# An SSD branch whose heads begin beside its convolution, in a two-layer hybrid encoder

## The chip, the cores and the metric

The kernel runs on one core of one Trainium2 chip. Its engines work side by side: TensorE (PE) multiplies matrices, VectorE (DVE) and ScalarE (ACT) work elementwise, GpSimd (POOL) does little here, and SyncE (SP) issues the transfers (DMAs). Each engine takes its instructions in a fixed order and waits where an operand is not there yet. The metric is the device time of one launch in microseconds (us), lower is better.

## What is computed

Two layers act on x of 512 tokens by 2048 features, in float32. Each one normalises, multiplies by one wide input matrix whose columns go to two branches, and multiplies the joined branches by one output matrix; a gate made from the conditioning vector scales the sum into x. The first layer (attention and S5) is not touched. The second, cut to what matters:

```python
h, gate = ada_modulate(x, c, norm_g, ada_w, ada_b)        # gate: a 2048 x 2048 product with silu(c)
q, k, v, g_c, z, xbc, dt_raw = split_cols(h @ w_in, ...)
o_c = neighbourhood_attention(q, k, v, rpb) * silu(g_c)   # 8 heads of 128
# SSD: 16 heads of 64, 2 groups of B and C with 128 states, chunks of 128 tokens, two directions
xbc = silu(depthwise_conv_centred(xbc, conv_w, conv_b))   # 5 taps, 1536 channels: x 1024, B 256, C 256
scores = einsum('bclhn,bcshn->bhcls', C, B) * exp(segsum(dt * a))
y_diag = einsum('bhcls,bcshp->bclhp', scores, x * dt)      # inside a chunk, head by head
states = ...                                               # B^T x per chunk, carried from chunk to chunk
y_off = einsum('bclhn,bchpn->bclhp', C, states) * exp(a_cum)
o_d = rms_norm((y_fwd + y_bwd + d * x) * silu(z), norm_w)
out = concat(o_c, o_d) @ w_out;  x = x + gate * out
```

## The kernel before

Every large product is done as three float32r matmuls: the operand and the weight are each split into a high and a low part, `wh` by a copy on ACT (L128), `wl` by a subtraction on DVE (L129). Weights come in pieces of 512 KB, in the order of a list (`plan1`), through two buffers `w` and three of `wh` and `wl`. PE works in units. A `tunit` is 48 matmuls of 128x512 (L167 to L169) into one of four banks `m`; a `runit` (L234 to L236) gives a whole 512x256 result.

Layer 1 issues: three runits for z and dt; twelve tunits for the convolution's channels (x0 to x7, B, C); eight tunits for the gate of the attention; then twelve runits, k, v and q of four pairs of heads; then sixteen output units. The runits of k, v and q read a reordered copy of h; its first tile is a copy into the buffer G11, high half on ACT (L1764), low half on DVE (L1765), and the others go into freed tiles of h.

Everything else is in streams, Python generators of which `slot` takes a step after every twelve or so matmuls. Their instructions are issued with raised priority, and a list scheduler of the framework, which knows the priorities and simulates times, fixes each engine's order when the kernel is built. The streams of layer 1:

- `ada_stream((3,), G[7:9])`: the gate of layer 1, 32 pieces of 512 KB through the two tiles G7 and G8, each multiplied and summed on DVE (L629). `finish("dt", "conv", "ada3")` ends it before the gate's tunits.
- `dt_stream`: step sizes, cumulative sums, and rows of decays, stored to DRAM (`csd`).
- `conv_stream`: for each of the twelve units five taps (L1322, L1325), tanh (L1330), a product (L1333), and for x and B transposes on PE (L1337) with a copy (L1339).
- `ssd`, started after all twelve units: `ssd_heads` loads a head's rows of decays (DMAs from `csd`), takes exponentials on ACT (L1392, L1394), multiplies on DVE (L1402, L1406 eight times, L1410) and multiplies by x on PE (L1416); `ssd_states` carries the states, per group of heads and per direction three steps of two PE products (L1446, L1455) with DVE products between them (L1443, L1451, L1452, L1458, L1459); `ssd_end` multiplies by the gate z (L1468), normalises, and stores the result to DRAM (`odd`).
- `na_stream`: the attention, one step a slot, which waits for the end of `ssd`.

After the last runit `odd` is loaded (L1796) and split, and the output units begin with the SSD half.

Of the kernel before, what the change touches and what calls it, by code (L numbers as in the profile page):

```python
# [66 lines left out]
class Trunk:  # L67
    def __init__(self, tc, ctx, A):
        self.tc, self.nc, self.A = tc, tc.nc, A
        self.sb = ctx.enter_context(tc.tile_pool(name="sb", bufs=1))  # L70
        self.pp = ctx.enter_context(tc.tile_pool(name="pp", bufs=1, space=PSUM))
        self.dr = ctx.enter_context(tc.tile_pool(name="dr", bufs=1, space=DRAM))
        self.uid = 0
        self.streams = []
        self.mrot = self.trot = 0
        self.nmain = 4
        self.sstep = 1
        self.flags = set()

    def nm(self, p):  # L80
# [23 lines left out]

    def slot(self, hold=()):
        for _ in range(self.sstep):
            for st in list(self.streams):
                if st[0] in hold:
                    continue
                for _ in range(st[2]):  # L110
                    with self.tc.high_priority(offset=PRI_BG):
                        r = next(st[1], "end")
                    if r == "end":
                        self.streams.remove(st)
                        self.flags.add(st[0])
                        break
# [1078 lines left out]
    def dt_stream(self, raw, G):  # L1195
# [29 lines left out]
        n = 8  # L1225
# [28 lines left out]
        for i, (part, at, al) in enumerate(((hi, 3, 4), (lo, 5, 6))):  # L1254
# [48 lines left out]
    def conv_stream(self, xins, G, xs):  # L1303
# [10 lines left out]
        acc = self.sl(G[9], [128, 2, 512])  # L1314
        tnh = self.sl(G[10], [128, 2, 512])
        for i in range(13):
            if i < 12:
                j = i
                yield from self.wait(f"xin{j}")
                xin = xins.pop(j)  # L1320
                a = acc[:, j % 2]
# [7 lines left out]
                tn = tnh[:, j % 2]  # L1329
                nc.scalar.activation(out=tn, in_=a, func=AF.Tanh)  # L1330
                dst = self.bT[:, j - 8] if 8 <= j < 10 else self.cT[:, j - 10] if j >= 10 else a
                yield
                nc.vector.scalar_tensor_tensor(out=dst, in0=tn, scalar=1.0, in1=a, op0=ALU.add, op1=ALU.mult)  # L1333
                if j < 10:
                    tp = self.bank("b3")
                    for t in range(4):
                        nc.tensor.transpose(tp[:, t * 128:t * 128 + 128], dst[:, t * 128:t * 128 + 128], self.ident)  # L1337
                    o = xs[:, :, j * 128:j * 128 + 128] if j < 8 else self.bs[:, :, (j - 8) * 128:(j - 8) * 128 + 128]
                    nc.scalar.copy(out=o, in_=tp.rearrange("p (t c) -> p t c", t=4))  # L1339
            yield  # L1340

    def ssd_heads(self, G, xs, ys):
# [42 lines left out]
        pd = None  # L1385
        for i in range(16 + 1):
            if i < 16:
                h = i
                r = rt[h].rearrange("p d (c l) -> p d c l", c=4)
                for d in range(2):  # L1390
# [5 lines left out]
                nc.scalar.activation(out=ys[:, :, x], in_=xs[:, :, x], func=AF.Identity, scale=self.ssd_dd[:, h:h + 1])  # L1396
            yield
            h = i - 1
            if h >= 0:
                e, lo = rt.pop(h), rl.pop(h)  # L1400
# [10 lines left out]
                load(h + 3)  # L1411
                if h % 2 == 0:
                    pd = self.bank("b1")
                for c in range(4):
                    o = (h % 2) * 256 + c * 64
                    nc.tensor.matmul(out=pd[:, o:o + 64], lhsT=wp[:, h % 2, c * 128:c * 128 + 128],  # L1416
                                     rhs=xs[:, c, h * 64:h * 64 + 64])
                if h % 2 == 1:
                    yo = ys[:, :, (h - 1) * 64:(h + 1) * 64].rearrange("p c (h x) -> p c h x", h=2)
                    v.tensor_tensor(out=yo, in0=pd.rearrange("p (h c x) -> p c h x", h=2, c=4), in1=yo, op=ALU.add)  # L1420
                    self.flags.add(f"yd{h // 2}")
            yield

    def ssd_states(self, G, xs, ys):

        nc = self.nc
        v = nc.vector
        dv = self.dtv
        xo = self.sl(G[10], [128, 2, 512])
        sp = self.sl(G[9], [128, 2, 512])  # L1430
        n = 0
        for g in range(2):
            yield from self.wait(f"yd{4 * g + 3}")
            for d in range(2):
                hs = slice(16 * d + 8 * g, 16 * d + 8 * g + 8)
                cols = slice(g * 512, g * 512 + 512)
                hv = lambda t: t.rearrange("p (h x) -> p h x", h=8)
                bc = lambda t: t.unsqueeze(2).to_broadcast([128, 8, 64])
                order = (0, 1, 2, 3) if d == 0 else (3, 2, 1, 0)
                for i in range(3):  # L1440
                    c, c2 = order[i], order[i + 1]
                    x = xo[:, 0]
                    v.tensor_tensor(out=hv(x), in0=hv(xs[:, c, cols]), in1=bc(dv["dec"][:, c, hs]), op=ALU.mult)  # L1443
                    yield
                    ps = self.bank("b2")
                    nc.tensor.matmul(out=ps, lhsT=self.bs[:, c, g * 128:g * 128 + 128], rhs=x)  # L1446
                    s, sl = sp[:, i % 2], sp[:, 1 - i % 2]
                    if i == 0:
                        nc.scalar.copy(out=s, in_=ps)
                    else:  # L1450
                        v.tensor_tensor(out=hv(s), in0=hv(sl), in1=bc(dv["etot"][:, c, hs]), op=ALU.mult)  # L1451
                        v.tensor_tensor(out=s, in0=s, in1=ps, op=ALU.add)  # L1452
                    yield
                    po = self.bank("b3")
                    nc.tensor.matmul(out=po, lhsT=self.cT[:, g, c2 * 128:c2 * 128 + 128], rhs=s)  # L1455
                    yield
                    o = xo[:, 1]
                    v.tensor_tensor(out=hv(o), in0=hv(po), in1=bc(dv["ecs"][:, c2, hs]), op=ALU.mult)  # L1458
                    v.tensor_tensor(out=ys[:, c2, cols], in0=ys[:, c2, cols], in1=o, op=ALU.add)  # L1459
                    n += 1  # L1460

# [192 lines left out]
    def layer1(self):  # L1654
# [72 lines left out]
        for j in range(12):  # L1727
            def ev(ps, j=j):
                t = self.sl(G[14 + j % 2], [128, 516])
                nc.gpsimd.memset(t[:, 0:2], 0.0)  # L1730
                nc.gpsimd.memset(t[:, 514:516], 0.0)
                nc.scalar.copy(out=t[:, 2:514], in_=ps)
                xins[j] = t
                self.flags.add(f"xin{j}")
            self.tunit(self.h_rhs, 16, ev)
        gc = self.scratch("gc", [8, 128, 512])
        self.gt_tile(G[17])
# [211 lines left out]
def plan1(A):  # L1949
# [30 lines left out]
```

## Time and profile before

| what | us |
|---|---|
| median of 3 runs (lowest, highest) | 1838.96 (1835.25, 1839.21) |
| the profiled execution | 1831.32 |
| its span, first to last instruction | 1829.5 |
| PE busy | 1770.3 (97%) |
| DVE busy | 1209.7 (66%) |
| ACT busy | 730.0 (40%) |

The profiled execution is 7.6 us shorter than the median of the runs. A matmul's busy time includes its way through the array, and the next one begins before it ends: 128x512 matmuls are recorded as 0.39 us and start 0.23 us apart. DVE's records overlap too, a little. So the tables of busy time are upper bounds, and lengths of work are read from one start to the next.

### The profile page before, as it was taken

To read this page: it belongs to the slowest core of one execution; us is meant where nothing else is said; L and a number is where in the kernel's file an instruction comes from. 1 tells how busy PE (TensorE), PEld (TensorE's weight loads), DVE (VectorE), ACT (ScalarE), POOL (GpSimd) and SP (SyncE) were. 2 spreads that over 40 slices of the span, in tenths; PEclk is the share of its full clock that TensorE was granted. 3 is DMA by queue.
4 is the path that set the end of the run, shared out by engine and by line. 5 is a ranking of instruction groups with operands and counts; after the bars stand their busy time and mean duration, and the time that the engine had idled before them with its cause. 6 is when DMAs were issued, how large, how long until landed. Compare 5 with 4: busy or idle time off the path is not lost.

```text
span 1829.5 us, 28824 instructions
## 1 busy us (share of the span) xinstructions
PE 1770.3 (97%) x11176; PEld 1522.8 (83%) x11176; DVE 1209.7 (66%) x2336; ACT 730.0 (40%) x1357; POOL 25.1 (1%) x44
## 2 busy tenths in 40 slices
PE   6899999899999989999999999999999999999999
PEld 3677897699989867888878878878799999997887
DVE  6897697984699999842256676589974453644332
ACT  6333454236235434432243244356644343442211
POOL 0000000000000000011100000000000000000000
PEclk8999999999999989999999999999999999999999
DMA  9997626747989887664435743358533333243542
GB/s 325 375 340 278 186 79 220 241 124 247 313 315 295 285 283 259 209 207 140 138 108 161 246 142 117 104 169 250 165 105 115 110 99 102 93 141 100 180 140 90
DMA packets 140906, 347.52 MB, mean 190 GB/s; under 512 B 31488, under 2 KB 42656, under 8 KB 140768
## 3 DMA queue, kind: packets, MB, share of 16 engines
q1 hardware_dynamic: 140768, 345.67, 57.6%
q8 instruction: 88, 1.44, 0.3%
q14 instruction: 50, 0.41, 0.1%
HBM read 310.48 MB, written 33.56 MB: 188 GB/s over the span
## 4 chain that ended last, share of the span: by engine, by line
PE 65%; DVE 16%; DMA 12%; issue 3%; ACT 1%; SPq 1%; DVEq 0%; ACTq 0%
PE m L167 10%; PE m L169 10%; PE m L168 10%; PE m L235 7%; PE m L234 7%; PE m L236 7%; DMA G<-in_ada_r_dram 6%; DVE G L629 3%; DVE wl L129 3%; PE b L169 2%; PE b L167 2%; PE b L168 2%; PE b L573 1%; PE b L973 1%; PE b L461 1%
## 5 line engine op out<-in xcount | busy, mean ns | idle before, releaser
L129 DVE TENSOR_TENSOR wl<-w,wh 128x1024 fp32r<-128x1024 f32 (+2 forms) x262 | 313.9, 1199 | 256.8 <-ACT wh L128 254.0
L128 ACT CAST wh<-w 128x1024 fp32r<-128x1024 f32 (+2 forms) x262 | 269.1, 1029 | 522.3 <-PE m L168 267.5
L168 PE MATMUL m<-H,wh 128*128 128x512 f32 (+1 forms) x968 | 381.9, 395 | 1.2 <-DVE H L992 1.2
L167 PE MATMUL m<-H,wh 128*128 128x512 f32 (+1 forms) x968 | 380.8, 398 | 2.2 <-ACT G L1144 2.1
L169 PE MATMUL m<-H,wl 128*128 128x512 f32 (+1 forms) x968 | 378.8, 396 | 2.2 <-DVE wl L129 2.2
L234 PE MATMUL m<-wh,H 128*128 128x256 f32 (+2 forms) x1232 | 353.3, 288 | 2.6 <-ACT H L665 1.5
L236 PE MATMUL m<-wh,H 128*128 128x256 f32 (+2 forms) x1232 | 353.8, 289 | 0.3 <-DVE H L1765 0.3
L235 PE MATMUL m<-wl,H 128*128 128x256 f32 (+2 forms) x1232 | 353.0, 287 | 0.2 <-DVE wl L129 0.2
L234 PEld LDWEIGHTS m<-wh,H 128*128 128x128 f32 x1232 | 233.8, 190 | 7.3 <-ACT H L665 2.6
L236 PEld LDWEIGHTS m<-wh,H 128*128 128x128 f32 x1232 | 233.4, 190 | 3.5 <-issue 1.0
L235 PEld LDWEIGHTS m<-wl,H 128*128 128x128 f32 x1232 | 234.0, 190 | 2.6 <-issue 0.7
L167 PEld LDWEIGHTS m<-H,wh 128*128 128x128 f32 x968 | 182.9, 190 | 46.0 <-issue 4.2
L169 PEld LDWEIGHTS m<-H,wl 128*128 128x128 f32 x968 | 181.8, 188 | 44.1 <-issue 3.5
L168 PEld LDWEIGHTS m<-H,wh 128*128 128x128 f32 x968 | 182.3, 188 | 42.4 <-issue 2.6
L629 DVE SCALAR_TENSOR_TENSOR G<-G,cb 128x1024 f32<-128x1024 f32 x128 | 155.0, 1220 | 55.5 <-DMA G<-in_ada_r_dram 47.7
L169 PE MATMUL m<-OLa,wl 128*128 128x512 f32 (+1 forms) x132 | 51.3, 389 | 0.6 <-DVE wl L129 0.5
L167 PE MATMUL m<-OLa,wh 128*128 128x512 f32 (+1 forms) x132 | 51.5, 390 | 0.2 <-ACT wh L128 0.2
L167 PE MATMUL m<-OLb,wh 128*128 128x512 f32 (+1 forms) x132 | 50.1, 388 | 1.4 <-ACT OLb L128 1.4
L167 PE MATMUL b<-H,wh 128*128 128x512 f32 x128 | 50.2, 406 | 0.8 <-DVE G L1045 0.8
L169 PE MATMUL m<-OLb,wl 128*128 128x512 f32 (+1 forms) x132 | 50.9, 386 | 0.0
L168 PE MATMUL m<-OLa,wh 128*128 128x512 f32 (+1 forms) x132 | 50.8, 385 | 0.0
L168 PE MATMUL m<-OLb,wh 128*128 128x512 f32 (+1 forms) x132 | 50.7, 384 | 0.0
(406 smaller groups left out, 2685.2 us busy)
## 6 DMA issues: line engine op xcount, KB each, us to landing
G<-in_ada_r_dram SPq DMA_DIRECT2D x128, 512.0 KB
w<-in_w_kvq_dram SPq DMA_DIRECT2D x72, 512.0 KB
w<-in_w_out_dram SPq DMA_DIRECT2D x64, 512.0 KB
w<-in_w_x_dram SPq DMA_DIRECT2D x36, 512.0 KB
OLa<-in_ada_dram SPq DMA_DIRECT2D x32, 512.0 KB
OLb<-in_ada_dram SPq DMA_DIRECT2D x32, 512.0 KB
G<-s_ck SPq DMA_DIRECT2D x32, 512.0 KB
s_ck<-G SPq DMA_DIRECT2D x16, 512.0 KB
```

What stands on the lines that cost most here:

```text
L128: self.nc.scalar.copy(out=hi, in_=src)
L129: self.nc.vector.tensor_tensor(out=lo, in0=src, in1=hi.bitcast(F32), op=ALU.subtract)
L167: mm(out=out, lhsT=lh, rhs=rh, start=start, stop=False)
L168: mm(out=out, lhsT=lh, rhs=rl, start=False, stop=False)
L169: mm(out=out, lhsT=ll, rhs=rh, start=False, stop=stop)
L234: mm(out=o, lhsT=hi, rhs=wh[:, c], start=(k == 0 and i % per == 0), stop=False)
L235: mm(out=o, lhsT=hi, rhs=wl[:, c], start=False, stop=False)
L236: mm(out=o, lhsT=lo, rhs=wh[:, c], start=False, stop=last)
L461: nc.tensor.matmul(out=xp[c][:, gg * 64:gg * 64 + 64], lhsT=gt[:, c, g], rhs=self.s5_u(b * 4 + g))
L573: nc.tensor.matmul(out=yp[:, cols], lhsT=ck[:, c, g], rhs=sts[:, j % 2, c, g], start=False, stop=(c == 1))
L629: nc.vector.scalar_tensor_tensor(out=t, in0=t, scalar=1.0, in1=cb, op0=ALU.mult, op1=ALU.mult, accum_out=o)
L973: nc.tensor.matmul(out=ps[32 * i:32 * i + 32, 0:256], lhsT=self.cs[:, 4 * q + i:4 * q + i + 1].to_broadcast([128, 32]), rhs=abuf[k][:, q, ...
```

## The change

The convolution takes B and C first (`CONV`), and its transposes come one round later. `ssd` is started together with `dt` and `conv`; its heads wait for the flags `dt` and `bc` (B and C done) and for the two heads' x (`xs0` to `xs7`), and a head's PE product comes one turn later. While the convolution's units run, `ssd` takes a step in every second slot. `ssd_states` waits for the whole convolution, and then works on both directions in turn, with buffers of their own (G10 and bank b2, G11 and bank b0). The gate's stream `ada3` begins after `ssd` in the program, with the tiles ropeq and ropek, which the heads' rows use before it. The rows of `dt_stream` move from G11 to G16, and the convolution's inputs from G14, G15 to G17, G11. The attention takes two steps a slot, and `odd` is loaded right after it is stored, into ropeq, ropek, r2k, w2k, H16 and H17. The numbers of operations on each engine stay as they were.

```diff
 def slot
+        self.turn += 1
...
-                if st[0] in hold:
+                if st[0] in hold or self.turn % self.every.get(st[0], 1):
                     continue
 def dt_stream
-            rt = self.sl(G[11], [32, 2, 512])
+            rt = self.sl(G[16], [32, 2, 512])
 def conv_stream
         for i in range(13):
+            if turn is not None:
+                j, dst = turn
...
+                    nc.tensor.transpose(tp[:, t * 128:t * 128 + 128], dst[:, t * 128:t * 128 + 128], self.ident)
...
+                self.flags.add(f"xs{j}")
+            turn = None
+            if i == 5:
+                self.flags.add("bc")
             if i < 12:
-                j = i
+                j = CONV[i]
...
                 if j < 10:
...
+                    turn = j, dst
 def ssd_heads
+        yield from self.wait("dt")
+        yield from self.wait("bc")
...
-        for i in range(16 + 1):
+        for i in range(16 + 2):
+            h = i - 2
+            if h >= 0:
...
+                    nc.tensor.matmul(out=pd[:, o:o + 64], lhsT=wp[:, h % 2, c * 128:c * 128 + 128],
+                                     rhs=xs[:, c, h * 64:h * 64 + 64])
             if i < 16:
                 h = i
+                yield from self.wait(f"xs{h // 2}")
 def ssd_states
+        yield from self.wait("conv")
-        xo = self.sl(G[10], [128, 2, 512])
+        xo = [self.sl(t, [128, 2, 512]) for t in (G[10], G[11])]
...
+        def chain(g, d):
...
+            x, o, s = xo[d][:, 0], xo[d][:, 1], sp[:, d]
+            for i in range(3):
...
+                ps = self.bank(("b2", "b0")[d])
+                nc.tensor.matmul(out=ps, lhsT=self.bs[:, c, g * 128:g * 128 + 128], rhs=x)
...
+                po = self.bank("b3")
+                nc.tensor.matmul(out=po, lhsT=self.cT[:, g, c2 * 128:c2 * 128 + 128], rhs=s)
+                yield
+                v.tensor_tensor(out=hv(o), in0=hv(po), in1=bc(dv["ecs"][:, c2, hs]), op=ALU.mult)
+                v.tensor_tensor(out=ys[:, c2, cols], in0=ys[:, c2, cols], in1=o, op=ALU.add)
...
+            live = [chain(g, 0), chain(g, 1)]
...
+            while live:
+                live = [t for t in live if next(t, "end") != "end"]
+                yield
 def layer1
-        self.start("ada3", self.ada_stream((3,), G[7:9]))
...
-        self.finish("dt", "conv", "ada3")
...
+        def ada3():
+            yield from self.wait("ssd")
+            yield from self.ada_stream((3,), ("ropeq", "ropek"))
+        self.every["ssd"] = 2
         self.start("ssd", ssd())
+        self.start("ada3", ada3())
+        for i, j in enumerate(CONV):
...
+                t = self.sl((G[17], G[11])[i % 2], [128, 516])
...
-        self.start("na", self.na_stream(T, raws, oc, gc))
+        self.start("na", self.na_stream(T, raws, oc, gc), 2)
...
-        of = [self.sl(f"H{16 + i}", [128, 512]) for i in range(8)]
+        self.finish("ada3")
+        of = []
+        for t in ("ropeq", "ropek"):
+            t = self.sl(t, [128, 2, 512])
+            of += [t[:, 0], t[:, 1]]
+        of += [self.sl(t, [128, 512]) for t in ("r2k", "w2k", "H16", "H17")]
```

`plan1` lists the convolution's weights in the order of `CONV`.

How the engines' orders move, at three places. Names carry running numbers; m, b are banks, G, H, OL, rope buffers, and line numbers of the changed kernel are some 4 to 40 higher than those of the kernel before.

PE where the last gate unit ends and the first runit of k begins, before: the runit (L234 to L236) follows at once, with a head's product (L1416) and a state's product (L1455) between its matmuls.

```order
L168 MATMUL m0_1574_11593<-H31_1264_9011,wh_1575_11594 128x512
L169 MATMUL m0_1574_11593<-H30_1263_9009,wl_1576_11595 128x512
L234 MATMUL m1_1590_11732<-wh_1584_11662,G11_1595_11740 128x256
L1416 MATMUL b1_1581_11630<-OLa_1308_9537,G8_1486_10738 128x64 x4
L1455 MATMUL b3_1603_11795<-G9_1485_10725,G5_1327_9614 128x512
L235 MATMUL m1_1590_11732<-wl_1585_11663,G11_1595_11740 128x256
```

So the heads' and states' products that were left then stood between matmuls of k.

The same place now (the runit is L238 to L240, the states' products are L1465 and L1476). Ahead of it stands an L1476 into b3_1552 and then eleven matmuls of the gate unit, the last of which is the first row here; seven state products follow alone.

```order
L173 MATMUL m0_1554_11621<-H30_1263_9009,wl_1556_11623 128x512
L1476 MATMUL b3_1559_11657<-G9_1480_10935,G5_1321_9601 128x512
L1465 MATMUL b2_1578_11750<-G10_1478_10933,G6_1322_9602 128x512
L1476 MATMUL b3_1563_11677<-G9_1480_10935,G5_1321_9601 128x512
L1476 MATMUL b3_1584_11790<-G9_1480_10935,G5_1321_9601 128x512
L1465 MATMUL b0_1597_11870<-G11_1479_10934,G6_1322_9602 128x512
L1476 MATMUL b3_1592_11831<-G9_1480_10935,G5_1321_9601 128x512
L1476 MATMUL b3_1609_11944<-G9_1480_10935,G5_1321_9601 128x512
L238 MATMUL m1_1566_11703<-wh_1560_11659,G11_1571_11711 128x256
```

No state product is left behind the first runit matmul, and that matmul reads G11, which the second direction's chain used until just before.

DVE, the low half of the first reordered tile (CAST into G11), before:

```order
L1289 TENSOR_TENSOR G12_1319_9568<-G12_1319_9568 128x128
L1298 TENSOR_TENSOR G12_1319_9568<-G12_1319_9568 128x128
L1765 CAST G11_1595_11740<-H1_1209_8728 128x512
L129 TENSOR_TENSOR wl_1388_10037<-w_1375_9930,wh_1387_10036 128x1024
L1322 TENSOR_SCALAR G9_1329_9616<-G15_1380_9982,convw_1320_9569 128x512
```

It stood ahead of the first convolution tap, long before any runit of k.

The same copy now (L1799): it is the last of 37 rows that begin with the L1478 which reads b3_1552; ten of them are pieces of `ada3` (L633), four the products with z (L1497), one a weight split (L133).

```order
L633 SCALAR_TENSOR_TENSOR ropek_1792_13598,adap_1662_12548<-ropek_1792_13598,cb_1752_13241 128x1024
L1478 TENSOR_TENSOR G10_1478_10933<-b3_1592_11831,G12_1315_9561 128x512
L1497 TENSOR_TENSOR OLb_1309_9538<-OLb_1309_9538,G1_1269_9056 128x1024
L633 SCALAR_TENSOR_TENSOR ropeq_1799_13636,adap_1662_12548<-ropeq_1799_13636,cb_1752_13241 128x1024
L1479 TENSOR_TENSOR OLb_1309_9538<-OLb_1309_9538,G10_1478_10933 128x512
L633 SCALAR_TENSOR_TENSOR ropek_1801_13672,adap_1662_12548<-ropek_1801_13672,cb_1752_13241 128x1024
L1478 TENSOR_TENSOR G11_1479_10934<-b3_1609_11944,G12_1315_9561 128x512
L1497 TENSOR_TENSOR OLb_1309_9538<-OLb_1309_9538,G3_1271_9058 128x1024
L1479 TENSOR_TENSOR OLb_1309_9538<-OLb_1309_9538,G11_1479_10934 128x512
L633 SCALAR_TENSOR_TENSOR ropeq_1809_13727,adap_1662_12548<-ropeq_1809_13727,cb_1752_13241 128x1024
L1497 TENSOR_TENSOR OLb_1309_9538<-OLb_1309_9538,G0_1268_9055 128x1024
L1799 CAST G11_1571_11711<-H1_1209_8728 128x512
```

DVE in the middle of the convolution now:

```order
L1430 TENSOR_TENSOR w2k_1383_10102<-w2k_1383_10102,G7_1377_10082 128x512
L1430 TENSOR_TENSOR ropek_1385_10108<-ropek_1385_10108,G7_1377_10082 128x512
L1341 SCALAR_TENSOR_TENSOR G9_1323_9603<-G17_1368_10004,convw_1316_9562,G9_1323_9603 128x512
L1434 SCALAR_TENSOR_TENSOR G14_1381_10098<-G14_1381_10098,G12_1315_9561,r2k_1382_10101 128x128 x4
L1434 SCALAR_TENSOR_TENSOR G15_1384_10105<-G15_1384_10105,G12_1315_9561,ropek_1385_10108 128x128 x2
L133 TENSOR_TENSOR wl_1390_10120<-w_1372_10013,wh_1389_10119 128x1024
```

Products of the first heads (L1430, L1434) stand around a tap (L1341); before, the heads' rows came behind the last tap. Of the 32 pieces of `ada3` the DVE order now holds all between the last head and the copy into G11; before, eight stood in the first layer and 24 between the layers' ends and the first convolution taps.

## Rows read from the trace of the kernel before

**Rows 1.** The page: busy time, share and instructions by engine.

```profile
PE 1770.3 (97%) x11176; PEld 1522.8 (83%) x11176; DVE 1209.7 (66%) x2336; ACT 730.0 (40%) x1357; POOL 25.1 (1%) x44
```

**Rows 2.** Waits of PE, 1038 to 1350 us: in total, times, longest.

```profile
PE m L169 <- DVE wl L129: 2.2, 1, 2.2
...
PE b L1416 <- DVE OLb L1420: 0.3, 1, 0.3
```

**Rows 3.** Busy time by stretch: PE, PEld, DVE, ACT, POOL, PEclk, DMA share, GB/s.

```profile
1038.00:1182.00 144.00, 140.89 (x643) 113.86 (x642) 96.48 (x155) 58.36 (x105) 1.31 (x20) 0.99 0.41 135
1182.00:1350.00 168.00, 161.83 (x847) 130.90 (x847) 147.36 (x296) 96.56 (x212) 0.00 (x0) 1.00 0.59 176
1042.70:1046.00 3.30, 3.30 (x9) 2.56 (x8) 2.50 (x4) 0.00 (x0) 0.00 (x0) 0.50 1.00 328
```

**Rows 4.** Timeline of PE: start, length; the first convolution unit, and after a wait.

```profile
1038.29 0.39 PE L167 MATMUL m<-H,wh 128*128 128x512 f32 x1
1038.51 0.40 PE L168 MATMUL m<-H,wh 128*128 128x512 f32 x1
1041.13 0.50 PE L169 MATMUL m<-H,wl 128*128 128x512 f32 x1 [2.23 <-DVE wl L129]
...
1043.04 0.63 PE L167 MATMUL m<-H,wh 128*128 128x512 f32 x1
1043.46 0.63 PE L168 MATMUL m<-H,wh 128*128 128x512 f32 x1
```

**Rows 5.** Timeline of PE: the first runit matmul of k; a state product there.

```profile
1303.32 0.28 PE L234 MATMUL m<-wh,G 128*128 128x256 f32 x1
...
1346.54 1.02 PE L1455 MATMUL b<-G,G 128*128 128x512 f32 x2
1347.00 0.68 PE L234 MATMUL m<-wh,H 128*128 128x256 f32 x1
```

**Rows 6.** PE products into the banks b, 1303 to 1350 us: first and last start.

```profile
L1416 PE MATMUL b<-OLa,G x32: 218/275/323, 1303.4 to 1319.5; 128*128 128x64 f32 x32
L1455 PE MATMUL b<-G,G x16: 591/592/648, 1304.3 to 1347.0; 128*128 128x512 f32 x16
L1446 PE MATMUL b<-G,G x12: 591/592/593, 1309.8 to 1341.6; 128*128 128x512 f32 x12
```

**Rows 7.** Line L629 on DVE, 1020 to 1066 us; then its timeline.

```profile
L629 DVE SCALAR_TENSOR_TENSOR G<-G,cb x16: 1218/1226/1229, 1020.0 to 1062.3; 128x1024 f32<-128x1024 f32 x16
...
1027.20 1.23 DVE L629 SCALAR_TENSOR_TENSOR G<-G,cb 128x1024 f32<-128x1024 f32 x1 [1.03 <-DMA G<-in_ada_r_dram]
...
1038.71 1.23 DVE L629 SCALAR_TENSOR_TENSOR G<-G,cb 128x1024 f32<-128x1024 f32 x1 [1.90 <-DMA G<-in_ada_r_dram]
1039.86 1.22 DVE L129 TENSOR_TENSOR wl<-w,wh 128x1024 fp32r<-128x1024 f32 x1
```

**Rows 8.** Timeline of DVE among the states' and heads' products.

```profile
1336.93 1.22 DVE L129 TENSOR_TENSOR wl<-w,wh 128x1024 fp32r<-128x1024 f32 x1
1338.06 0.68 DVE L1443 TENSOR_TENSOR G<-OLa,G 128x512 f32<-128x512 f32 x1
1338.66 0.68 DVE L1458 TENSOR_TENSOR G<-b,G 128x512 f32<-128x512 f32 x1
...
1218.67 2.19 DVE L1406 SCALAR_TENSOR_TENSOR G<-G,G,ropek 128x128 f32<-128x128 f32 x8 [0.52 <-ACT G L1394]
```

**Rows 9.** Waits of DVE, 1182 to 1350 us.

```profile
DVE ropek L1402 <- DMA ropek<-csd: 4.2, 5, 1.8
DVE r2k L1402 <- DMA r2k<-csd: 2.9, 3, 1.9
DVE w2k L1402 <- DMA w2k<-csd: 1.9, 2, 1.5
```

**Rows 10.** Waits of PE, 1640 to 1700 us.

```profile
PE m L167 <- ACT OLb L128: 1.4, 1, 1.4
PE b L167 <- DVE H L1650: 0.9, 1, 0.9
```

More of the change, by code (lines that the diff above doesn't have):

```diff
@@ L26 @@
 HEAD = 1
+CONV = (8, 9, 10, 11) + tuple(range(8))
 PRI_B = 3000
@@ L78, in __init__ @@
         self.flags = set()
+        self.turn = 0
+        self.every = {}
     def nm(self, p):
@@ L1315, in conv_stream @@
         tnh = self.sl(G[10], [128, 2, 512])
+        turn = None
         for i in range(13):
+            if turn is not None:
+                j, dst = turn
+                tp = self.bank("b3")
+                for t in range(4):
+                    nc.tensor.transpose(tp[:, t * 128:t * 128 + 128], dst[:, t * 128:t * 128 + 128], self.ident)
+                o = xs[:, :, j * 128:j * 128 + 128] if j < 8 else self.bs[:, :, (j - 8) * 128:(j - 8) * 128 + 128]
+                nc.scalar.copy(out=o, in_=tp.rearrange("p (t c) -> p t c", t=4))
+                self.flags.add(f"xs{j}")
+            turn = None
+            if i == 5:
+                self.flags.add("bc")
             if i < 12:
-                j = i
+                j = CONV[i]
                 yield from self.wait(f"xin{j}")
                 xin = xins.pop(j)
-                a = acc[:, j % 2]
+                a = acc[:, i % 2]
                 nc.vector.tensor_scalar(out=a, in0=xin[:, 0:512], scalar1=cw[:, j, 0:1], scalar2=cw[:, j, 5:6],
@@ L1334, in conv_stream @@
                 if j < 10:
[L1335 to L1339, printed above, removed]
+                    turn = j, dst
             yield
@@ L1385, in ssd_heads @@
         pd = None
-        for i in range(16 + 1):
+        for i in range(16 + 2):
+            h = i - 2
+            if h >= 0:
+                if h % 2 == 0:
+                    pd = self.bank("b1")
+                for c in range(4):
+                    o = (h % 2) * 256 + c * 64
+                    nc.tensor.matmul(out=pd[:, o:o + 64], lhsT=wp[:, h % 2, c * 128:c * 128 + 128],
+                                     rhs=xs[:, c, h * 64:h * 64 + 64])
             if i < 16:
                 h = i
+                yield from self.wait(f"xs{h // 2}")
                 r = rt[h].rearrange("p d (c l) -> p d c l", c=4)
@@ L1397, in ssd_heads @@
             yield
+            h = i - 2
+            if h >= 0 and h % 2 == 1:
+                yo = ys[:, :, (h - 1) * 64:(h + 1) * 64].rearrange("p c (h x) -> p c h x", h=2)
+                v.tensor_tensor(out=yo, in0=pd.rearrange("p (h c x) -> p c h x", h=2, c=4), in1=yo, op=ALU.add)
+                self.flags.add(f"yd{h // 2}")
             h = i - 1
-            if h >= 0:
+            if 0 <= h < 16:
                 e, lo = rt.pop(h), rl.pop(h)
@@ L1411, in ssd_heads @@
                 load(h + 3)
[L1412 to L1421, printed above, removed]
             yield
@@ L1432, in ssd_states @@
         for g in range(2):
             yield from self.wait(f"yd{4 * g + 3}")
[L1434 to L1460, printed above, removed]
@@ L1462, in ssd_end @@
+            live = [chain(g, 0), chain(g, 1)]
+            next(live[0])
+            next(live[0])
+            next(live[0])
+            while live:
+                live = [t for t in live if next(t, "end") != "end"]
+                yield
     def ssd_end(self, G, ys, z):
@@ L1747, in ssd, with ev @@
             yield from self.ssd_end(G, ys, zt)
+        def ada3():
+            yield from self.wait("ssd")
+            yield from self.ada_stream((3,), ("ropeq", "ropek"))
+        self.every["ssd"] = 2
         self.start("ssd", ssd())
+        self.start("ada3", ada3())
+        for i, j in enumerate(CONV):
+            def ev(ps, j=j, i=i):
+                t = self.sl((G[17], G[11])[i % 2], [128, 516])
+                nc.gpsimd.memset(t[:, 0:2], 0.0)
+                nc.gpsimd.memset(t[:, 514:516], 0.0)
+                nc.scalar.copy(out=t[:, 2:514], in_=ps)
+                xins[j] = t
+                self.flags.add(f"xin{j}")
+            self.tunit(self.h_rhs, 16, ev)
+        gc = self.scratch("gc", [8, 128, 512])
+        self.every = {}
+        self.gt_tile(G[17])
         for j in range(8):
@@ L1956, in plan1 @@
         t = A[n]
-        p += [t[i, j] for i in range(t.shape[0]) for j in range(t.shape[1])]
+        p += [t[i, j] for i in (CONV if n == "w1_x" else range(t.shape[0])) for j in range(t.shape[1])]
     p += out_pieces(A["w1_out"], 1)
```

32 lines of the change are left out of this document (19 added, 13 removed).

## The prediction

> **What bounds the kernel now.** First the page: PE is busy 97% of the span, DVE 66%, ACT 40% [rows 1]. So the time falls only where a wait of PE goes, and rises where one comes. Next the list of PE's waits from the first convolution unit to the middle of k, 1038 to 1350 us: nine waits of 2.2 down to 0.3 us, one each, 9.4 us together [rows 2]; the longest is for a weight split on DVE. Then the table by stretch: DVE is busy 96.5 of 144 us in the first part and 147.4 of 168 in the second, where the heads, the states and the gate units lie together [rows 3]. The timelines then give prices. PE's 128x512 matmuls start 0.22 to 0.23 us apart (1038.29, 1038.51); after the 2.2 us wait two start 1041.13 - 1038.51 = 2.62 us apart, 0.16 more than wait and pitch together [rows 4]. From 1042.70 the granted clock is 0.50, the level of 1.2 GHz [rows 3], and matmuls start 0.42 us apart [rows 4]: eight of them cost 8 x 0.2 = 1.6 us. DVE: a product of 128x512 takes 0.60 us (1338.06 to 1338.66), a weight split 1.13, an L629 piece 1.15 (1038.71 to 1039.86), eight L1406 2.19 [rows 7, 8]. A state's product on PE is two instructions, 0.46 us to the next start and a slow next one (0.68 for 0.28), so 0.86 us [rows 5].
>
> **What the change removes.** The 2.2 us wait is DVE's: an `ada3` piece waited 1.90 us for its DMA, and the weight split stood behind it [rows 7]. With `ada3` gone from there it goes, with its half clock. The states' and heads' waits go too: all of their products now lie among gate units, and four heads and the states, which PE still had at 1303 to 1347 us beside k [rows 6], come earlier. That work stays the same in number (32 L1416; 28 state instructions), so only waits count: 9.4 + 9 x 0.16 = 10.8, with 1.6 of half clock **12.4 us**. At the end of the attention PE waits 1.4 + 0.9 us and less than that three times [rows 10]. The two steps a turn put the transposes among more matmuls; I take 1.1 off (bounds 0 to 2.3); the 1.4, a split of the last head on ACT, stays.
>
> **What it adds.** The first reordered tile, hp[0], lies in G11, and G11 is now also the second direction's buffer in `ssd_states`. Before, its copy on DVE stood ahead of the convolution. Now it is behind the last L1479 that reads G11, and the first matmul of k reads it. On PE, an L1476 into b3_1552 is followed by eleven gate matmuls and seven state products, and then by that first matmul. On DVE, from the L1478 that reads b3_1552 to the copy there are 37 rows: ten `ada3` pieces x 1.15 = 11.5; four products with z, 128x1024 like a split, x 1.14 = 4.6; one split, 1.1; 21 of 128x512 x 0.60 = 12.6; the copy, some 0.3. Together 30.2 us, with no wait in it. The L1478 can't start before its L1476 has ended. PE meanwhile has 11 x 0.23 + 7 x 0.86 = 8.6 us to do. So PE waits at least **21.6 us**, whichever of those rows it meets first.
>
> Four terms come on top, each bounded by rows:
> - Waits of DVE for `ada3` DMAs inside this stretch. There are two tiles in both versions, and in the trace a tile comes round in 5.6 us (16 pieces from 1020.0 to 1062.3, that is 2.8 us apart) [rows 7]. Now ten pieces share 30.2 us, 3.0 apart, unevenly. Bounds 0 and 6 (ten at 0.6); I take 2.5. The Trainium skill, page "DMA: Bandwidth & Descriptors", section "Anatomy of one DMA", gives about 2.0 us plus the bytes over 436 GB/s for a GpSimd-issued transfer; an estimate from it for 512 KB is 3.2 us, a round of 4.35 with the piece itself, so no wait here, and the sum would be 2.5 lower. The row, 5.6, disagrees with it, and decides.
> - DVE late when the stretch begins. From the first head's product to the first state's product the DVE order's rows come to 124 us by these pitches; PE has 529 of the 960 gate and convolution matmuls there. Before, those 960 and what lies between took 1303.3 - 1038.3 - 12.4 = 252.6 us, 0.263 each, so 139 us: DVE leads by 15. Waits for the rows of decays were 4.2 + 2.9 + 1.9 = 9 us [rows 9]. In the next stretch 21 `ada3` pieces stand among 57 us of DVE work against 59 of PE; at half a us of DMA wait each (between 0 and the 1.03 and 1.90 shown [rows 7]) that is 10. 15 - 9 + 2 - 10 = -2: late by 2 (0 to 10).
> - Half clock after the long wait: as after the 2.2 us wait 1.6 [rows 3, 4]; bounds 0 and 3.4, twice that.
> - Refilling, the copy on ACT, and the next tiles of h, which come only as fast as DVE copies them: 1.0 (0 to 3).
>
> **What costs nothing, with its cover.** B and C first changes only the weights' order. The convolution's inputs in G17 and G11, and `rt` in G16, make a tile wait for its second last user; four banks `m` cover that. The transposes a round later and a head's product a turn later wait less; if the 15 us lead is gone, they wait for DVE as the states do. `ada3`: its 32 pieces are 37 us of DVE work, its 32 DMAs of 512 KB leave SP's queue at 742 to 779 and 977 to 1062 us, and join it at the gate units, where the DMA engines are busy 0.59 [rows 3]; the weights issued behind them have three `wh`, `wl` and two `w` as cover, and what that fails to cover is in the first term. `odd` is loaded right behind each store: SP waits there for the store to land, and k's weights are queued behind it; the five pieces ahead cover 12 matmuls each, and if they didn't it costs up to 3 us. The earlier end of the states lets `na` begin earlier, which lies beside PE's runits as before.
>
> **The sum.** 21.6 + 2.5 + 2 + 1.6 + 1.0 = 28.7 of new waits, less 12.4 and 1.1: **+15.2 us**. The profiled execution would go from 1831.3 to 1846.5; the median shown stands 7.6 above it, so 1854. The bounds: all low, 21.6 - 13.5 = +8, 1847; all high, 21.6 + 6 + 10 + 3.4 + 3 - 13.5 = +30.5, 1869.5.
>
> **The rivals.**
> - Worse: `ada3` starves PE before the gate's end. If each of the first 21 pieces waits 1.5 us, the mean of the two waits shown [rows 7], DVE loses 31 us; less the lead of 15, 16 go through to PE, where 2 are counted: +14, **1868**. For it: DVE has 147 of 168 us of work there already, and `wl` stands behind each piece. Against it: the pieces are as far apart as a tile's round allows.
> - Faster: DVE is so far ahead that the copy into G11 ends with the last gate matmul. Then only the 13.5 are left: **1825**. It decides at the last L1479 that reads G11: it would have to be done within some 3 us of the last state product, and the products with z and the ten pieces to be done earlier. Against it: the order on each engine is fixed, and the L1478 can't pass its L1476.
> - No difference: the stretch is half as long, because PE met the L1476 early (it too stands in a row of chained products, and where PE waits there for DVE, DVE runs ahead among its pieces). A wait of 12 to 14 us cancels the gain: **1839**.
> - That the heads don't begin earlier is excluded by the order: L1434 stands around the taps of the convolution.
>
> **Chances.** The forecast 0.66, worse 0.22, no difference 0.07, faster 0.05. 0.2% is 3.7 us, about what a measurement of this kernel can tell from no change; so slower by more than that is 0.88. The range takes the bounds of the sum and a little toward the no-difference case: 1844 to 1870.
>
> **What would show it.** In the profile after: one wait of PE above 20 us at the first matmul of k (L238), or divided between it and the state products just ahead, for hp[0]'s copy (L1798, L1799), near 1310 to 1340 us, with the granted clock low behind it; the waits of [rows 2] gone; DVE busier from 1100 to 1182 than the page's slices show before. I am wrong if that matmul waits below 10 us, or if the largest wait is elsewhere, at a weight split behind an `ada3` piece.

## The result, and the profile after

The changed kernel takes 1850.73 us (median of 4 runs, 1847.71 to 1854.26) against 1837.11 before (4 runs, 1833.76 to 1839.21): a ratio of 1.0083, 95% interval 1.006 to 1.0106, or 13.6 us more. The forecast was 1854, in a range of 1844 to 1870, and slower with a chance of 0.88. The profiled execution of after is the first of its four runs, 1853.33 us.

The page of after: the span, the busy time by engine, and of the 40 slices those of PE and of its granted clock.

```profile
span 1851.5 us, 28812 instructions
...
PE 1779.9 (96%) x11176; PEld 1529.4 (83%) x11176; DVE 1206.5 (65%) x2336; ACT 729.0 (39%) x1357; POOL 25.2 (1%) x44
...
PE   6999999999999989999999999999599999999999
...
PEclk8999999999999989999999999999699999999999
```

The instructions of each engine are as many as in [rows 1], and DVE has no more to do. One slice, the 29th (1296 to 1342 us), stands out: PE is half idle there, and the granted clock is at 0.6. Nearly all of the loss lies in it. The list of PE's waits of after, 1038 to 1370 us (in total, times, longest):

```profile
PE b L1476 <- DVE G L1478: 11.1, 4, 4.3
PE m L238 <- ACT G L1798: 5.8, 1, 5.8
PE b L1476 <- DVE G L1471: 3.9, 1, 3.9
PE b L1465 <- DVE G L1471: 1.4, 1, 1.4
PE b L1465 <- DVE G L1460: 1.0, 1, 1.0
PE m L240 <- DVE G L1799: 0.3, 1, 0.3
```

That is 23.5 us. The weight split's wait of [rows 2] is gone, and of the heads and states one of 1.0 us is left ahead of 1300 us, at 1254 (L1465); all the others come after 1300. PE's timeline from the end of the gate to k (start, length, the wait before it):

```profile
1302.11 1.13 PE L1476 MATMUL b<-G,G 128*128 128x512 f32 x2 [1.17 <-DVE G L1478]
...
1310.05 2.07 PE L1476 MATMUL b<-G,G 128*128 128x512 f32 x2 [4.25 <-DVE G L1478]
1313.47 2.08 PE L1465 MATMUL b<-G,G 128*128 128x512 f32 x2 [1.35 <-DVE G L1471]
1315.34 1.92 PE L1476 MATMUL b<-G,G 128*128 128x512 f32 x2
1321.19 2.05 PE L1476 MATMUL b<-G,G 128*128 128x512 f32 x2 [3.93 <-DVE G L1471]
...
1332.67 2.07 PE L1476 MATMUL b<-G,G 128*128 128x512 f32 x2 [2.98 <-DVE G L1478]
1340.59 0.58 PE L238 MATMUL m<-wh,G 128*128 128x256 f32 x1 [5.84 <-ACT G L1798]
...
1346.54 0.28 PE L238 MATMUL m<-wh,H 128*128 128x256 f32 x1
```

The first row is the L1476 into b3_1552, the row at 1310.05 the first of the seven that stand alone. The gaps between them all come from one stretch of DVE. Its timeline shows that stretch from the L1478 that reads b3_1552 to the copy into G11, the CAST L1799, and the row behind it:

```profile
1309.31 0.69 DVE L1478 TENSOR_TENSOR G<-b,G 128x512 f32<-128x512 f32 x1
...
1322.25 1.23 DVE L633 SCALAR_TENSOR_TENSOR ropeq<-ropeq,cb 128x1024 f32<-128x1024 f32 x1 [1.21 <-DMA ropeq<-in_ada_r_dram]
...
1339.37 1.22 DVE L633 SCALAR_TENSOR_TENSOR ropeq<-ropeq,cb 128x1024 f32<-128x1024 f32 x1
1340.51 1.22 DVE L1497 TENSOR_TENSOR OLb<-OLb,G 128x1024 f32<-128x1024 f32 x1
1341.65 0.41 DVE L1799 CAST G<-H 128x512 fp32r<-128x512 f32 x1
1341.98 1.22 DVE L633 SCALAR_TENSOR_TENSOR ropek<-ropek,cb 128x1024 f32<-128x1024 f32 x1
```

From start to start that is 1341.98 - 1309.31 = 32.7 us, for 37 rows. The last row is a piece of `ada3`, the 32nd: so 31 of the 32 pieces stand ahead of the copy, not all of them. In the stretch DVE waits 2.3 us, for DMAs of `ada3` alone:

```profile
DVE ropeq L633 <- DMA ropeq<-in_ada_r_dram: 1.5, 2, 1.2
DVE ropek L633 <- DMA ropek<-in_ada_r_dram: 0.8, 2, 0.4
```

The table by stretch of after (columns as in [rows 3]): DVE is busier from 1038 to 1182, 111.7 us for 96.5, as the heads moved there; from 1300 to 1350 PE works only 27.5 of 50 us. In the last row the granted clock is 0.50, its level of 1.2 GHz.

```profile
1038.00:1182.00 144.00, 144.00 (x700) 119.33 (x699) 111.70 (x221) 75.22 (x163) 1.24 (x18) 1.00 0.50 158
1182.00:1300.00 118.00, 117.00 (x530) 91.72 (x529) 105.09 (x195) 55.26 (x107) 0.13 (x2) 1.00 0.73 234
1300.00:1350.00 50.00, 27.49 (x85) 15.45 (x84) 46.53 (x92) 14.29 (x24) 0.00 (x0) 0.62 0.58 181
1310.00:1341.00 31.00, 14.16 (x16) 4.26 (x17) 28.75 (x45) 4.39 (x8) 0.00 (x0) 0.50 0.73 224
```

### The profile page after: what moved, and what is told of

It is laid out like the page before. It is cut to its first block, busy times and chain, and to the rows that moved or that the text cites. A ratio compares the mean times of both kernels' runs of the same rounds, so it can differ in the third digit from the quotient of the medians.

```text
span 1851.5 us, 28812 instructions
## 1 busy us (share of the span) xinstructions
PE 1779.9 (96%) x11176; PEld 1529.4 (83%) x11176; DVE 1206.5 (65%) x2336; ACT 729.0 (39%) x1357; POOL 25.2 (1%) x44
## 4 chain that ended last, share of the span: by engine, by line
PE 70%; DVE 14%; DMA 9%; ACT 3%; issue 3%; SPq 1%; DVEq 0%; ACTq 0%
PE m L171 10%; PE m L173 10%; PE m L172 10%; PE m L240 8%; PE m L238 8%; PE m L239 8%; PE b L173 2%; PE b L171 2%; PE b L172 2%; DVE wl L133 2%; DMA ropeq<-in_ada_r_dram 2%; PE b L577 1%; PE b L977 1%; PE b L465 1%; DVE w2k L487 1%
## 5 line engine op out<-in xcount | busy, mean ns | idle before, releaser
L133 DVE TENSOR_TENSOR wl<-w,wh 128x1024 fp32r<-128x1024 f32 (+2 forms) x262 | 314.0, 1200 | 283.5 <-ACT wh L132 280.8
L171 PE MATMUL m<-H,wh 128*128 128x512 f32 (+1 forms) x968 | 381.4, 398 | 2.2 <-ACT G L1148 2.1
L173 PE MATMUL m<-H,wl 128*128 128x512 f32 (+1 forms) x968 | 378.8, 396 | 0.0
L238 PE MATMUL m<-wh,H 128*128 128x256 f32 (+2 forms) x1232 | 353.4, 287 | 2.5 <-DVE r2k L895 1.4
L240 PE MATMUL m<-wh,H 128*128 128x256 f32 (+2 forms) x1232 | 353.4, 287 | 0.0
L238 PEld LDWEIGHTS m<-wh,H 128*128 128x128 f32 x1232 | 234.6, 191 | 5.2 <-DVE r2k L895 1.8
L240 PEld LDWEIGHTS m<-wh,H 128*128 128x128 f32 x1232 | 234.5, 191 | 1.7
L171 PEld LDWEIGHTS m<-H,wh 128*128 128x128 f32 x968 | 183.1, 190 | 46.8 <-issue 4.7
L173 PEld LDWEIGHTS m<-H,wl 128*128 128x128 f32 x968 | 182.3, 189 | 42.7 <-issue 4.6
L633 DVE SCALAR_TENSOR_TENSOR G<-G,cb 128x1024 f32<-128x1024 f32 x96 | 115.9, 1217 | 21.4 <-DMA G<-in_ada_r_dram 15.6
L171 PE MATMUL m<-OLb,wh 128*128 128x512 f32 (+1 forms) x132 | 50.8, 388 | 1.4 <-ACT OLb L132 1.4
L171 PE MATMUL m<-OLa,wh 128*128 128x512 f32 (+1 forms) x132 | 51.5, 390 | 0.2 <-ACT wh L132 0.2
L173 PE MATMUL m<-OLa,wl 128*128 128x512 f32 (+1 forms) x132 | 51.1, 387 | 0.5 <-DVE wl L133 0.5
L173 PE MATMUL m<-OLb,wl 128*128 128x512 f32 (+1 forms) x132 | 50.9, 386 | 0.0
L171 PE MATMUL b<-H,wh 128*128 128x512 f32 x128 | 49.8, 402 | 0.8 <-DVE G L1049 0.8
```

What stands on the lines that cost most here:

```text
L133: self.nc.vector.tensor_tensor(out=lo, in0=src, in1=hi.bitcast(F32), op=ALU.subtract)
L171: mm(out=out, lhsT=lh, rhs=rh, start=start, stop=False)
L173: mm(out=out, lhsT=ll, rhs=rh, start=False, stop=stop)
L238: mm(out=o, lhsT=hi, rhs=wh[:, c], start=(k == 0 and i % per == 0), stop=False)
L240: mm(out=o, lhsT=lo, rhs=wh[:, c], start=False, stop=last)
L633: nc.vector.scalar_tensor_tensor(out=t, in0=t, scalar=1.0, in1=cb, op0=ALU.mult, op1=ALU.mult, accum_out=o)
```

## The experiments

The theory: PE waits because hp[0] shares G11 with the second direction's chain, so that k can't begin, and the chain's products stand alone, until DVE has worked through what is queued ahead of the copy; without that the change would gain what it was counted to remove. Rivals: the pieces of `ada3` on DVE are the cost and the buffer incidental; the early heads cost elsewhere what they save; or `ada3`'s leaving its old place gave the whole gain. The table has times and ratios to before (95% interval), with the waits of PE from 1010 to 1350 us in the profile. Each kernel is compared with the runs of before that were made beside it:

| kernel | median us (runs) | ratio to before | waits, us |
|---|---|---|---|
| before, beside the first four | 1834.58 (18) | | 9.4 |
| chain in G7 | 1822.69 (6) | 0.9933 (0.9918 to 0.9947) | 1.5 |
| ada3 in k | 1842.24 (7) | 1.0038 (1.0023 to 1.0054) | 12.7 |
| both | 1823.15 (6) | 0.9934 (0.9919 to 0.9950) | 0 |
| before, ada3 in k | 1838.76 (12) | 1.0023 (1.0010 to 1.0035) | 4.2 |
| before, beside the next four | 1833.97 (7) | | |
| change, again | 1850.86 (4) | 1.0086 (1.0066 to 1.0106) | 21.8 |
| attention one step a slot | 1849.26 (4) | 1.0080 (1.0062 to 1.0098) | 23.6 |
| chain in G7, old conv order | 1824.45 (4) | 0.9948 (0.9927 to 0.9968) | 4.2 |
| chain in G7, one direction | 1823.17 (4) | 0.9941 (0.9918 to 0.9964) | 4.1 |

To find where a kernel gains or loses, the 8688 matmuls of L167 to L169 and L234 to L236 (in after four lines higher) can be counted off: they come in nearly the same order in all these kernels (some change places among themselves, but as many of each kind lie ahead of the numbers below), so the same number marks the same amount of work. The table gives the shift of a number's start against the trace of before, in us, with that of number 4304 (1029.8 us in before, ahead of the convolution) taken off. The numbers are: 4600, in the convolution; 6000, at 1406 us in before, behind the heads and states of every kernel; 8688, the last.

| kernel | 4600 | 6000 | 8688 |
|---|---|---|---|
| the change; again | -6.0; -6.0 | +21.0; +19.0 | +19.8; +17.8 |
| chain in G7 | -6.0 | -11.9 | -12.8 |
| ada3 in k | -6.0 | +9.6 | +10.0 |
| both | -6.0 | -10.8 | -9.3 |
| before, ada3 in k | -5.5 | -7.7 | +5.0 |
| attention one step a slot | -6.0 | +21.0 | +20.3 |
| chain in G7, old conv order | -6.0 | -7.7 | -8.9 |
| chain in G7, one direction | -6.0 | -7.8 | -9.1 |

**The chain in G7.** The second direction's chain gets G7 in place of G11. G7 holds the first group's decay mask, last read for the eighth head, and is free from there on.

```diff
-        xo = [self.sl(t, [128, 2, 512]) for t in (G[10], G[11])]
+        xo = [self.sl(G[10], [128, 2, 512])]
...
             yield from self.wait(f"yd{4 * g + 3}")
+            if g == 0:
+                xo.append(self.sl(G[7], [128, 2, 512]))
```

> The changed kernel with one buffer moved: the second direction's chain works in G7, free after the eighth head, instead of G11. The copy of the first reordered tile into G11 then stands early on DVE, and the first matmul of k stands ahead of the last six state products on PE; ada3 stays where the change put it. My theory (PE waits because hp[0] can't be written before the chain has left G11): the 21 to 24 us of wait at the gate's end go, and in their place come the few us by which DVE is late in the next stretch. From the L1478 that reads b3_1552, 48 rows of DVE are 12 pieces of ada3, 3 products with z, 4 weight splits, 12 copies and some 18 of 128x512, about 37 us, against about 34 us of PE; so 3 us, with bounds 0 and 8. Time some 20 us below the changed kernel, 1830 (1825 to 1837), ratio to before 0.993 to 1.000. Rival (the ada3 pieces on DVE are the cost, the buffer is incidental): DVE's work is the same, so PE still waits 15 us or more, time 1842 to 1850.

Measured: 1822.69 us, 0.9933 of before. The wait list of PE, 1010 to 1370 us, is one row; the copy into G11 (here L1801) starts at 1239.0 us, k (L238) at 1301.8; and the row of the table by stretch from 1300 us is the last one here:

```profile
PE b L1476 <- DVE G L1478: 1.5, 1, 1.5
```

```profile
L1801 DVE CAST G<-H x1: 421/421/421, 1239.0 to 1239.0; 128x512 fp32r<-128x512 f32 x1
...
L238 PE MATMUL m<-wh,G x8: 274/283/283, 1301.8 to 1326.5; 128*128 128x256 f32 x8
```

```profile
1300.00:1350.00 50.00, 48.52 (x363) 44.60 (x362) 46.34 (x76) 16.62 (x37) 0.00 (x0) 1.00 0.70 220
```

DVE is as busy as in the change, 46.3 us for 46.5, and the pieces of `ada3` are where they were (they start from 1237.9 to 1342.7 us, in the change from 1243.7 to 1342.0): the rival falls. The time is 7 us below the 1830 that was expected, and below its range of 1825 to 1837; the ratio lies in its range. I had taken only the waits off. In the change the seven state products and the first matmuls of k ran at half clock too, by the rows above an estimated 7 x (1.87 - 0.86) + 2.6 = 9.7 us of PE's time; and before itself ran 2.5 us lower beside this kernel. Moving one buffer turns 0.83% slower into 0.67% faster. No version run here has a lower median, but the next one and the one with one direction after the other, at 1823.15 and 1823.17 us, can't be told from it.

**`ada3` among k, v and q.** Each load is queued on SP behind the weight load issued last.

```diff
-                nc.sync.dma_start(out=tiles[i], in_=A["ada_r"][pieces[i]])
+                with self.tc.issue_after(self.wd[self.wi - 1].ins) if groups == (3,) else nullcontext():
+                    nc.sync.dma_start(out=tiles[i], in_=A["ada_r"][pieces[i]])
...
-            yield from self.wait("ssd")
+            yield from self.wait("kvq")
...
         self.start("na", self.na_stream(T, raws, oc, gc), 2)
+        self.flags.add("kvq")
```

> The changed kernel with the loads of ada3 tied behind the weight loads of k, v and q; G11 stays shared. On DVE 3 pieces of ada3 are left between the first L1479 that reads a state product behind the gate's last matmul and the copy into G11: 3 x 1.15 + 4 products with z x 1.14 + one split 1.14 + 13 of 128x512 x 0.60 = 17 us, against 4 state products on PE, 3.4. My theory: PE waits 13 to 14 us there instead of 23.5, and the low clock is shorter; time some 12 us below the changed kernel, 1839 (1835 to 1843), no better than before. Rival (the ada3 pieces are the cost): the wait goes nearly whole, time 1825 to 1831.

Waits of PE, 1290 to 1350 us:

```profile
PE b L1477 <- DVE G L1479: 5.7, 2, 4.2
PE b L1477 <- DVE G L1472: 4.8, 1, 4.8
PE m L238 <- ACT G L1799: 2.2, 1, 2.2
```

12.7 us, against 13 to 14 expected; the granted clock was 0.50 for 17 us, in the change for 38. So the pieces lengthen the stretch, here by nearly half of the wait, but what makes PE wait for it is the buffer. The time lies in the range expected; against before it is 7.7 us more, where 2 were expected: behind the stretch, in k, v and q, 6.3 us are lost again between matmuls 5800 and 6000, at a wait of 4.4 us (L1570) with a low clock. DVE waits 18.6 us for `ada3`'s DMAs between 1350 and 1430 us there, and 5.3 for `cb`.

**Both.**

> Both edits of the two kernels before: the chain in G7 and ada3 among k, v and q. My theory: no wait above 2 us is left between the convolution and k, and the 12.4 us that the change was to remove, with 1.1 at the attention's end, are gained against the kernel before: 1825 (1822 to 1830), ratio 0.991 to 0.996. Rival (heads beside the convolution cost as much elsewhere, in DVE or DMA collisions, as they save): 1834 or more.

1823.15 us, as expected, and no better than the chain in G7 alone. There is no wait left up to 1350 us; later come 2.1, 1.2 and 1.2 us (L1518, L171, L1628) in k, v and q. The rival, 1834 or more, falls: of the 13.5 us counted, 11.4 are gained, so the early heads don't cost elsewhere what the change saves.

**Before, with `ada3` among k, v and q.** The same tie of the loads, the stream's start moved behind `ssd`, its end ahead of the output units.

```diff
-        self.start("ada3", self.ada_stream((3,), G[7:9]))
...
-        self.finish("dt", "conv", "ada3")
+        self.finish("dt", "conv")
...
         self.start("na", self.na_stream(T, raws, oc, gc))
+        def ada3():
+            yield from self.wait("ssd")
+            yield from self.ada_stream((3,), ("ropeq", "ropek"))
+        self.start("ada3", ada3())
...
+        self.finish("ada3")
         self.out_units(o_rhs, out_evict, lambda: self.finish("na"))
```

> The kernel before with nothing changed but ada3, whose loads go behind those of the weights of k, v and q. My theory: the 2.2 us wait and its low clock go, 4.0 us together; the states' waits of 5 to 7 us stay, since they come from the products of a chain one after the other: 1833 (1830 to 1836), ratio 0.996 to 0.999. Rival (ada3's place is worth the whole gain, the early heads nothing): as fast as the kernel with both edits, 1825 or below.

A miss: 1838.76 us, a ratio of 1.0023, where 1833 (1830 to 1836) was expected. The table of shifts says why. Up to matmul 6000 it gains 7.7 us, more than the 4.0 expected, and then loses 12.7. The longest wait of PE, 1350 to 1500 us, and DVE's waits up to 1490:

```profile
PE b L1541 <- DVE G L1544: 5.7, 1, 5.7
```

```profile
DVE ropeq L630 <- DMA ropeq<-in_ada_r_dram: 13.3, 10, 2.8
DVE ropek L630 <- DMA ropek<-in_ada_r_dram: 10.9, 9, 2.1
```

DVE's timeline ahead of that wait's end:

```profile
1474.77 1.23 DVE L630 SCALAR_TENSOR_TENSOR ropek<-ropek,cb 128x1024 f32<-128x1024 f32 x1 [1.50 <-DMA ropek<-in_ada_r_dram]
...
1477.43 1.23 DVE L630 SCALAR_TENSOR_TENSOR ropeq<-ropeq,cb 128x1024 f32<-128x1024 f32 x1 [1.43 <-DMA ropeq<-in_ada_r_dram]
...
1480.51 1.23 DVE L630 SCALAR_TENSOR_TENSOR ropek<-ropek,cb 128x1024 f32<-128x1024 f32 x1 [1.84 <-DMA ropek<-in_ada_r_dram]
...
1484.59 0.74 DVE L1544 SCALAR_TENSOR_TENSOR G<-b,wqk,G 128x512 fp32r<-128x512 f32 x1
```

DVE has time there, but its order is fixed: L1544, which empties a bank of the attention, stands behind three pieces that each wait for a DMA. PE then stood 5.7 us, and the granted clock was 0.50 for 6.8 us from 1482.2. With the 4.1 us of smaller waits in the same list (2.4, 1.4 and 0.3; before has none there) that is about what is lost behind matmul 6000. `ada3` wants a place where nothing that PE waits for is queued behind its loads, not just an idle engine. The last rival is answered in part: with `ada3` in this new place the kernel as a whole is 0.2% slower. But up to matmul 6000 `ada3`'s leaving its old place brings by itself 7.7 of the 11.9 us that the chain in G7 has gained there.

**The change again.**

> The changed kernel once more, for a second profile and a comparison beside the next ones. My theory: again 21 to 26 us of waits of PE between 1295 and 1345 us, all at the states' products and the first matmul of k, granted clock low for 30 to 40 us there, ratio to before 1.006 to 1.010. Rival (the waits fell elsewhere by chance in the first profile): waits in other places, or below 15 us.

Ratio 1.0086; 21.8 us of waits, all at L1476, L1465, L238 and L240, and the granted clock 0.50 for 6.8 and 27.3 us between 1304 and 1342. It is the same picture.

**The attention at one step a slot.**

```diff
-        self.start("na", self.na_stream(T, raws, oc, gc), 2)
+        self.start("na", self.na_stream(T, raws, oc, gc))
```

> The changed kernel with the attention at one step a slot, as before. My theory: only the 1.1 us at the attention's end is given back: the 0.9 us wait for L1650's tile is there again between 1640 and 1720 us, time 1 us over the changed kernel (0 to 2.3). Rival (two steps a turn cost DVE or PE something in k, v and q): no wait returns, or the time falls.

1849.26 us, a ratio of 1.008 against 1.0086: no difference that can be told. The wait list of PE from 1620 to 1720 us:

```profile
PE m L171 <- ACT OLb L132: 1.4, 1, 1.4
PE m L173 <- DVE wl L133: 0.4, 1, 0.4
```

A miss: the 0.9 us wait of [rows 10] does not return, so it wasn't the two steps that removed it. That no wait returns was the sign of the rival, but a cost of the two steps isn't shown either. In the kernel before with `ada3` alone moved it is there (0.9, L1651). Which of the other edits removes it is open.

**The old order of the convolution, chain in G7.** `bc` is then set at the last round.

```diff
-CONV = (8, 9, 10, 11) + tuple(range(8))
+CONV = tuple(range(12))
...
-            if i == 5:
+            if i == 12:
```

> The kernel with the chain in G7, but the convolution in its old order, B and C last, so that the heads begin behind it as before; ada3 still follows the heads, and so reaches into k. My theory: the early heads are worth what the kernel with ada3 alone moved did not gain, 4 to 6 us, and ada3 among k, v and q costs some more by its waits for DMAs: 1827 to 1836, ratio to before 0.995 to 1.000. Rival (B and C first is worth nothing, ada3's place gave it all): 0.992 to 0.994, as with the chain in G7.

**One direction after the other, chain in G7.**

```diff
-            live = [chain(g, 0), chain(g, 1)]
-            next(live[0])
-            next(live[0])
-            next(live[0])
-            while live:
-                live = [t for t in live if next(t, "end") != "end"]
+            for d in range(2):
+                yield from chain(g, d)
                 yield
```

> The kernel with the chain in G7, but the second direction begins only when the first has ended, as before; all else of the change stays. My theory: the waits of the state products for each other come back, 1.8 + 1.7 + 1.1 + 0.7 us in the kernel before, now between matmuls of k: 3 to 6 us over the kernel with the chain in G7, ratio to before 0.995 to 0.997. Rival (PE has enough other matmuls between a chain's products, the turn is worth nothing): same time, 0.993.

The first took 1824.45 us, faster than the 1827 to 1836 expected; the second 1823.17, a ratio of 0.9941, a little faster than the 0.995 to 0.997 expected. Their waits of PE, 1010 to 1450 us, first of the old order, then of one direction:

```profile
PE b L1465 <- DVE G L1471: 2.1, 2, 1.6
PE m L239 <- DVE wl L133: 1.6, 1, 1.6
PE b L1407 <- DVE G L1438: 0.5, 1, 0.5
```

```profile
PE b L1476 <- DVE G L1471: 2.1, 1, 2.1
PE b L1465 <- DVE G L1460: 1.4, 1, 1.4
PE b L1476 <- DVE G L1478: 0.6, 1, 0.6
PE b L1513 <- ACT G L1514: 0.5, 1, 0.5
```

In the traces each part is worth some 4 us (-8.9 and -9.1 at the last matmul, against -12.8), and waits at the states come back in both, as the theory has it. But the trace of the chain in G7 is of its quickest run, 1819.71 us, and that of the old order of its slowest, 1827.76; and the ratios of the medians, 0.9948, 0.9941 and 0.9933, stand with intervals that overlap, so that the rivals, which put these parts at nothing, are not excluded. That the early heads and the two directions in turn each bring about 4 us is what three single traces show, not what the times prove.

## Why the prediction was right

- **What the change removes** (12.4, and 1.1 at the end, 13.5 together): the chain in G7 keeps nearly all of it, with one wait of 1.5 us left: -12.8 in the trace, 1834.58 - 1822.69 = 11.9 in the medians. Of its parts 6.0 us lie ahead of matmul 4600: 4.2 at the 2.2 us wait with its half clock (the shift at matmul 4400; 4.0 were counted), most of the rest at the 0.9 us wait of the same stretch. At the end of the attention 1 us went, as said, but not by the two steps named.
- **The new wait for G11** (at least 21.6): the stretch on DVE was put at 30.2 us without waits (the terms listed add up to 30.1), 32.7 with the 2.5 for `ada3`'s DMAs. It took 32.7, with 2.3 of waits. The estimate from the Trainium skill, page "DMA: Bandwidth & Descriptors", section "Anatomy of one DMA", whose figures are for a GpSimd-issued transfer, was a round of 4.35 us and so no wait there. The trace disagrees, with 2.3 us of waits, as the 5.6 us of [rows 7] did; these transfers are issued by SP.
- **DVE late** (2, bounds 0 to 10): too small. The L1476 into b3_1552 ends at 1302.11 + 1.13 = 1303.24, and the L1478 that reads it starts at 1309.31, 6.1 later. Of what made it late the prediction counted 19 us of waits, 9 for the rows of decays and 10 for `ada3`'s DMAs. DVE's list from 1110 to 1302 us comes to 19.6, but for other reasons:

```profile
DVE wl L133 <- ACT wh L132: 6.6, 4, 3.8
DVE ropeq L633 <- DMA ropeq<-in_ada_r_dram: 3.7, 4, 2.1
DVE ropeq L633 <- DMA cb<-cbd: 3.6, 1, 3.6
DVE ropeq L1434 <- ACT ropeq L1417: 3.0, 1, 3.0
DVE ropek L633 <- DMA ropek<-in_ada_r_dram: 1.2, 1, 1.2
...
DVE ropek L1430 <- DMA ropek<-csd: 0.4, 1, 0.4
```

  The rows of decays cost 0.4 us, `ada3`'s pieces 4.9, ACT some 10, and 3.6 went to the load of `cb`, the second half of the vector that `ada3` multiplies by, which the prediction did not count. That the total agrees is luck.
- **The state products' cover** (8.6): PE's waits from 1303 on are 21.3 us and not 26, since a state product at the low clock took 1.87 us from start to start (1313.47 to 1315.34) and not 0.86. Here that cost nothing by itself: DVE sets the end, and the products only fill more of the waiting.
- **Half clock behind it** (1.6): from 1340.59 to 1346.54 matmuls of k start 0.21 us apart, then 0.12: of 5.95 us 2.6 are lost, more than the 1.6 counted and within its bounds (of which the upper, "twice that", is 3.2 and not 3.4). In the whole the granted clock was 0.50 for 37.6 us from 1308.98. Of the refilling (1.0) the one wait of 0.3 us at L240 is all that shows.
- **The sum** (+15.2): in the two traces +19.8 and +17.8, in the medians +13.6 and, beside the later runs of before, +16.9. With the terms as the trace has them (DVE late by 6.1, half clock 2.6, refilling 0.3, 12.8 removed) the sum would be +20.3, near the traces. The trace of before is of a quick execution: 1831.3 against medians of 1834 to 1837, with single runs from 1826.9 to 1839.9. So the mechanism and its size were right, but that 1854 lies within 4 us of the median is in part chance.
- **The signs**: the wait came divided between the state products and k's first matmul, 21.3 us in all, and DVE is busy 73.8 of 82 us from 1100 to 1182, for 50.6 before. But L238 itself waited only 5.8 us, and a wait below 10 us there was also given as a sign of being wrong. That sign was badly put: the prediction had allowed for the wait to be divided.
- **The rivals**: a weight split behind an `ada3` piece starving PE did not come: no L173 is in the list of waits. The faster case, 1825, came as soon as G11 was not shared, 1822.69; its condition, the copy done when the gate ends, is met there by some 60 us (1239.0 against 1301.8), by another order on DVE and not by a faster DVE. A wait half as long, which was to cancel the gain, came only with 12.7 us in the kernel with `ada3` in k, and its time was not that of before, for the loss behind it.

## What to carry to other kernels

When a change gives a helper stream a buffer of its own, look up who takes that buffer next and on which engine's queue the first write stands: the price is what the fixed order puts ahead of that write, counted from the last instruction of the other engine that it depends on, less what that engine still has to do. Work moved to an idle stretch of an engine costs nothing only if no result that the busy engine needs is queued behind its transfers. Undo a suspected wait by moving one buffer before judging the rest of a change.

## What was not expected of the hardware

The low clock came with the waits and stretched the work between them: at a granted clock of 0.50 (1.2 GHz) a state product took 1.87 us, for 0.86 at 1.00. In the first trace of the change the clock came back at 1346.5, when PE had run without a gap since 1342.12. In the second it came back once in between, for 3.4 us from 1310.8, and fell again. Where PE waited 12.7 us in pieces, with `ada3` in k, it was low for 17.1 us; where it waited 1.5 us at once, with the chain in G7, it did not fall in that stretch at all.
